# Attention scores in one five-bank tile, the low part of the queries by halves of TensorE's rows

## The chip, the cores and the metric

One core of one Trainium2 chip runs the whole kernel. The metric is the device time of one launch in microseconds (us). The kernel before took 2810.9 us (median of three runs, 2809.32 to 2814.49). The launch that the hardware profiler recorded took 2803.03 us; its span, from the first to the last instruction, is 2801.1 us.

## The reference, cut to what matters

The kernel is one layer of a diffusion backbone: a token mixer (differential attention beside a bidirectional Mamba-2 scan), and after it a mixture of experts. The change lies in the attention and in what stands next to it. There are 1024 latent tokens as queries, 1280 keys (256 context tokens and the 1024), 8 heads, and for each head two softmaxes with keys of 64 numbers:

```python
s = einsum('bqhcd,bkhcd->bchqk', q, k) * ATTN_SCALE      # c: the two softmaxes, d: 64
p = softmax(s, axis=-1)
w = p[:, 0] - lam * p[:, 1]
o = einsum('bhqk,bkhd->bqhd', w, v)                      # d: 128
o = o * rsqrt(mean(o * o) + EPS) * g_subln * (1.0 - lam_init)
...
ya = o_attn @ w_branch_attn
ys = y_ssd @ w_branch_ssd
out = (g_a * ya + g_s * ys) @ w_out
```

All of it is float32. The kernel keeps that accuracy with TensorE's faster fp32r form by splitting a number into a high part (what fp32r holds) and a low part (the rest): a product of two such numbers is taken as high times high, high times low and low times high.

## The kernel before

The program is one long stream that a planner writes when the kernel is built (class `Flow`, from line 106). Every piece of work is a generator that yields what it waits for: tiles, free buffers of a ring, an engine, or a condition. `Flow.run` keeps a modelled clock for each engine and each buffer, and always lets go on the stream with the lowest priority number that could start by then. Each engine then executes its instructions in the order in which they were written; on the chip semaphores guard the data alone. So the modelled durations settle the order, and the chip settles the times.

**Queries and keys (`norm_and_qkv`, `post_qk`).** After the projection, each two token tiles are transposed, split in high and low (`sa`, `sb`), and stored to memory as `qk`, [head and softmax, 128 rows, 2T + NT columns], T = 1024 and NT = 1280. The rows are twice the 64 numbers of a key. The first T columns hold the high part of the queries in both halves, the next T columns their low part in both halves, and the last NT columns the keys: high part in the upper half of the rows, low part in the lower. A query pair of tiles takes eight stores, all from SyncE's queue.

**Attention (`attention`, from line 1342).** A head has eight tiles of 128 queries. `main` goes through 32 pairs of tiles, four to a head, in the order of `PLAN`: `S` is a softmax's scores for one query tile, `t` a group of four transposes of finished weights, `v` a step of the product with the values. A pair's scores run two pairs ahead of its transposes (`LEAD`), and the last two `v` lag by one more.

`scores` computes one softmax of one query tile in three pieces of 512, 512 and 256 keys. Each piece has its own bank from the ring `sps` (four banks), and takes two matmuls over all 128 rows: the queries' high part against the keys (high and low at once, by the two halves of the rows), and their low part against the same. `piece` has VectorE read the bank, scale it and write it to `e`, with the minimum of the piece as a by-product; `soft` joins the three minima (`red`), has ScalarE take the exponential with its sum, and after the second softmax has VectorE do a reciprocal, a small product and the combination of both softmaxes (`stt`, 1280 columns).

`attention_ahead` loads the stored `qk`, one tile of 1664 KB for each softmax of a head, into a ring of three, from GpSimd's queue. A tile goes back to the ring with the last query tile of its head.

**The branch products (`branches`, from line 1194).** The merged projections of both branches are 32 outputs of [128, 512], each a sum of 24 matmuls (8 chunks, three products of parts). The stream has the lowest priority, and so stands wherever the planner saw TensorE wait for something. The first 16 outputs (`ssd`) are spread over the attention: output n is not begun before `PACE[n]` pairs are done. The other 16 (`attn`) need the attention's results, and so come after it. All take their banks from the ring `bacc` (two banks), which `norm`, the attention's own normalisation once a head, uses too. `gated` multiplies an `ssd` output by its gate and stores it; `merge` does so for `attn` and adds the two.

**What follows.** `merge_and_out` zeroes a result buffer by stores from a tile of zeros and does the output projection, the router and the experts.

Names in the profile: `sps<-qk` scores, `e<-sps` VectorE's reads, `tr<-cst,e` transposes, `pv<-wr,vv` the product with the values, `bacc<-bx...` branch products, `bacc<-cst` the normalisation's. Line 147 is the matmul of the helper `mm`, 151 that of `tp`; a line can be a helper's.

Of the kernel before, what the change touches and what calls it, by code (L numbers as in the profile page):

```python
# [19 lines left out]
P = 128  # L20
D = 1024
KC = 8
# [12 lines left out]
PLAN = "S0 t0 v3'|S1 t1 v4' t2|S2 v0 t3 v1|S3 t4 v2"  # L35
# [339 lines left out]
class Layer:  # L375
# [114 lines left out]
    def norm_and_qkv(s):  # L490
# [5 lines left out]
        s.qk = [s.dram(f"qk{j}", [8, P, 2 * T + NT]) for j in range(2)]  # L496
# [163 lines left out]
        def post_qk(ps, kind, j, t):  # L660
# [36 lines left out]
            if two[2] == 2:  # L697
                o0 = (t // 2 - (kind == "q")) * 2 * P
                dst = s.qk[j].rearrange("(m u) (v x) c -> v u x m c", u=2, v=2)
# [494 lines left out]
    def branches(s):  # L1194
# [9 lines left out]
        whs, wls = s.ring(op, [P, 4, P], "bwh", 3, F32R), s.ring(op, [P, 4, P], "bwl", 3, F32R)  # L1204
# [42 lines left out]

        def main():
            for n, (kind, h) in enumerate(todo):
                for m in range(8):  # L1250
                    if kind == "ssd":
                        yield [lambda: st["pairs"] >= PACE[8 * n + m]]
                    yield [acc]
                    b = acc.get()
                    for k in range(KC):
                        yield [lambda: (kind, h, k) in xs and (kind, h, m, k // 4) in ws]
                        (xh, xl), (wh, wl) = xs[kind, h, k], ws[kind, h, m, k // 4]
                        yield [xh, F.ready[_n(xl)] + SLACK[5], wh, wl]
                        s.mm3(b, wh[:, k % 4], wl[:, k % 4], xh, xl, k == 0, k == KC - 1)
                        if k % 4 == 3:  # L1260
                            whs.put(wh)
                            wls.put(wl)
                        if m == 7:
                            xhs.put(xh)
                            xls.put(xl)
                    F.spawn(3, (gated if kind == "ssd" else merge)(h, m, b))

        def gated(h, m, b):
# [6 lines left out]
            acc.put(b)  # L1275
# [3 lines left out]
        def merge(h, m, b):  # L1279
# [9 lines left out]
            acc.put(b)  # L1289
# [34 lines left out]
    def attention_ahead(s, go):  # L1324
# [3 lines left out]
        s.qks, s.heads = s.ring(qp, [P, 2 * T + NT], "qk", 3, F32R), {}  # L1328

        def loads():  # L1330
            yield [go]
            for h in range(8):
                for c in range(2):
# [8 lines left out]
    def attention(s):  # L1342
        tc, nc, F = s.tc, s.nc, s.F
        ap, pp = s.open("at"), s.open("aps", True)
        if True:
            S = s.ring(pp, [P, 512], "sps", 4)
            TR = s.ring(pp, [P, 512], "tr", 1)
            PV = s.ring(pp, [P, 512], "pv", 1)
            acc = s.acc
# [16 lines left out]
            def main():  # L1366
# [5 lines left out]
                for p in range(len(pairs) + LEAD + 1):  # L1372
                    for j in range(4):
# [6 lines left out]
            def scores(h, qp, j, state):  # L1380
# [4 lines left out]
                qt, c = 2 * qp + j // 2, j % 2  # L1385
                if c == 0:
                    yield [es, sts]
                    w = state.setdefault((h, qp), [[], [], [], {}, []])
                    w[0].append(es.get())
                    w[4].append(sts.get())  # L1390
                e, st = state[h, qp][0][-1], state[h, qp][4][-1]
                tq = slice(qt * P, (qt + 1) * P)
                yield [lambda: (h, c) in heads]
                qk = heads[h, c]
                qa, qb, ks = qk[:, :T], qk[:, T:2 * T], qk[:, 2 * T:]
                got = []
# [6 lines left out]
                F.spawn(1, soft(e, st, s0[:, qt:qt + 1], c, got, state[h, qp][1]))  # L1403
                if qt == 7:
                    qks.put(qk)

            def piece(e, m, sps, n, got):
                yield [sps, "DVE"]
                F.ts_reduce(e, sps[:, :n], -0.125, ALU.mult, ALU.min, m)
                S.put(sps)  # L1410
                got.append(1)

            def soft(e, st, s0, c, got, flags):
                yield [lambda: len(got) == 3, "DVE"]
                F.red(st[:, 6 + c:7 + c], st[:, 3 * c:3 * c + 3], ALU.min)
# [57 lines left out]
            def norm(h, ot, s0):  # L1473
                yield [s0, "DVE"]
                F.stt(s0, s0, EPS, s0, ALU.mult, ALU.mult)
                yield [acc]
# [15 lines left out]
                for half in range(2):  # L1492
                    sl = slice(half * 512, half * 512 + 512)
                    yield [F.ready[_n(r)] + SLACK[3], acc]
# [983 lines left out]
```

## Time and profile before

| | |
|---|---|
| median of three runs | 2810.9 us (2809.32 to 2814.49) |
| the profiled execution | 2803.03 us, span 2801.1 us |
| TensorE's matmuls (PE) busy | 2618.4 us, 93% |
| its weight loads (PEld) | 2101.6 us, 75% |
| VectorE (DVE) | 2008.3 us, 72% |
| ScalarE (ACT) | 1339.9 us, 48% |
| GpSimd (POOL) | 888.9 us, 32% |
| mean granted TensorE clock | 0.974 |

Times inside the execution count from the span's start. The attention's scores run from 1053.9 to 1476.4, and the last matmul of the branch products starts at 1633.2. A matmul's duration in the profile is from its start to its modelled end, and holds a tail in which the next one already runs: what it costs on a busy engine is the step from its start to the next start. VectorE's durations overlap in the same way by a little. A group of instructions of one form is printed with its number, the union of their times, the mean of one, and the engine's idle time before them.

### The profile page before, as it was taken

How to read it: one execution, taken by the hardware profiler on the slowest of the kernel's cores; microseconds unless marked ns; L12 is line 12 of the kernel's file. 1: busy time of each engine (PE TensorE's matmuls, PEld its weight loads, DVE VectorE, ACT ScalarE, POOL GpSimd, SP SyncE). 2: the span in 40 equal slices, each digit the busy share in tenths (PEclk: the TensorE clock that was granted, in tenths of full speed). 3: DMA queues.
4: the chain of work that ended last, by engine and by line, in shares of the span. 5: the costliest groups of instructions: out<-in, count | busy, mean ns of one | idle time of the engine just before them, and what ended most of it. 6: DMA issues, size and time to landing. Idle time of an engine off the chain costs nothing. (4 is left out here: it accounts for less than half of the span.)

```text
span 2801.1 us, 41274 instructions
## 1 busy us (share of the span) xinstructions
PE 2618.4 (93%) x14561; PEld 2101.6 (75%) x14561; DVE 2008.3 (72%) x4690; ACT 1339.9 (48%) x2104; POOL 888.9 (32%) x671
## 2 busy tenths in 40 slices
PE   7999999999999999999999999899999998999891
PEld 4888778778787777888887787688878776776660
DVE  6877123768686749888894767877888877788753
ACT  4211123344444546666764422345666665666641
POOL 0111010545353520000000000065666656567641
PEclk9999999999999999999999999999999999999995
DMA  7767253243334354233234953478899999999997
GB/s 279 221 208 214 67 142 105 67 137 91 121 91 132 106 168 149 81 106 131 88 101 135 292 181 142 170 265 248 293 311 315 312 275 278 301 315 315 317 305 202
DMA packets 275123, 544.63 MB, mean 194 GB/s; under 512 B 31531, under 2 KB 166804, under 8 KB 247907
## 3 DMA queue, kind: packets, MB, share of 16 engines
q1 hardware_dynamic: 238754, 435.05, 45.5%
q0 software_dynamic: 36160, 106.93, 15.1%
q8 instruction: 115, 1.88, 0.3%
q14 instruction: 94, 0.76, 0.1%
HBM read 432.73 MB, written 124.73 MB: 199 GB/s over the span
## 5 line engine op out<-in xcount | busy, mean ns | idle before, releaser
L170 DVE TENSOR_TENSOR gl<-raw,gh 128x1024 fp32r<-128x1024 f32 x240 | 288.1, 1218 | 39.4 <-ACT gh L163 39.4
L147 PE MATMUL acc<-hh,hi 128*128 128x512 f32 (+2 forms) x760 | 304.8, 401 | 1.3 <-DVE ux L186 1.3
L163 ACT CAST gh<-raw 128x1024 fp32r<-128x1024 f32 x240 | 247.5, 1050 | 95.7 <-PE gu L147 63.2
L147 PE MATMUL acc<-hl,hi 128*128 128x512 f32 (+2 forms) x760 | 289.4, 381 | 0.0
L147 PE MATMUL acc<-hh,lo 128*128 128x512 f32 (+1 forms) x736 | 281.0, 382 | 3.0 <-DVE lo L170 3.0
L147 PE MATMUL gu<-gh,xh 128*128 128x512 f32 (+3 forms) x672 | 279.5, 416 | 3.3 <-ACT xh L163 3.0
L147 PE MATMUL gu<-gl,xh 128*128 128x512 f32 (+3 forms) x672 | 265.6, 395 | 4.5 <-DVE gl L170 4.4
L147 PE MATMUL gu<-gh,xl 128*128 128x512 f32 (+3 forms) x672 | 265.7, 395 | 0.5 <-DVE xl L170 0.5
L192 DVE TENSOR_SCALAR_CACHE_REDUCE e<-sps 128x512 f32<-128x512 f32 (+1 forms) x384 | 214.4, 597 | 29.5 <-PE sps L147 29.2
L261 POOL DMA_INDIRECT cr<-cumd,crow x98 | 118.9, 1213 | 312.5 <-DVE crow L186 280.9
L267 POOL DMA_INDIRECT yacc<-y,tk x98 | 184.4, 1881 | 84.5 <-issue 31.4
L147 PE MATMUL sps<-qk 128*128 128x512 f32 (+1 forms) x768 | 195.3, 386 | 8.2 <-DVE e L192 4.8
L155 ACT ACTIVATE e<-e,st 128x1280 f32<-128x1280 f32 x128 | 174.8, 1366 | 31.7 <-DVE st L201 31.5
L261 POOL DMA_INDIRECT wc<-wtab,tk x98 | 143.7, 1466 | 137.7 <-DVE tk L181 101.1
L147 PE MATMUL acc<-hi,hh 128*128 128x512 f32 x448 | 181.1, 404 | 0.0
L147 PE MATMUL acc<-hi,hl 128*128 128x512 f32 x448 | 176.1, 393 | 0.4 <-DVE hl L170 0.4
L147 PE MATMUL acc<-lo,hh 128*128 128x512 f32 x448 | 175.8, 392 | 0.0
L147 PEld LDWEIGHTS sps<-qk 128*128 128x128 f32 x768 | 140.9, 191 | 40.8 <-DVE e L192 9.8
L147 PEld LDWEIGHTS acc<-hh,hi 128*128 128x128 f32 (+1 forms) x760 | 142.5, 187 | 32.7 <-issue 4.2
L147 PE MATMUL pv<-wr,vv 128*128 128x256 f32 x640 | 164.2, 380 | 0.0
L147 PEld LDWEIGHTS acc<-hh,lo 128*128 128x128 f32 x736 | 138.8, 189 | 32.8 <-DVE lo L170 4.0
L147 PEld LDWEIGHTS acc<-hl,hi 128*128 128x128 f32 (+1 forms) x760 | 142.6, 188 | 27.4 <-issue 0.8
(326 smaller groups left out, 6254.8 us busy)
## 6 DMA issues: line engine op xcount, KB each, us to landing
raw<-in_w_e_gate_dram SPq DMA_DIRECT2D x64, 1024.0 KB, 8.6
raw<-in_w_e_up_dram SPq DMA_DIRECT2D x64, 1024.0 KB, 12.4
draw<-in_w_e_down_dram SPq DMA_DIRECT2D x64, 1024.0 KB, 10.8
qk<-qk POOLq DMA_DIRECT2D x16, 1664.0 KB, 11.1
raw<-in_w_in_dram SPq DMA_DIRECT2D x40, 512.0 KB, 4.7
wada<-in_w_ada_dram SPq DMA_DIRECT2D x32, 512.0 KB, 5.5
R<-acd SPq DMA_DIRECT2D x64, 256.0 KB, 5.3
qk<-sa SPq DMA_DIRECT2D x52, 256.0 KB, 4.0
```

The costliest lines, as they stand in the source:

```text
L147: s.nc.tensor.matmul(out, l, r, start=start, stop=stop)
L155: s.nc.scalar.activation(out, in_, fn, **kw)
L163: s.nc.scalar.copy(out, in_)
L170: s.nc.vector.tensor_tensor(out, a, b, op=op)
L192: s.nc.vector.tensor_scalar(out, a, s1, None, op0=op0, op1=op1, accum_out=acc)
L261: s.nc.gpsimd.indirect_dma_start(out=out, out_offset=None, in_=table, in_offset=bass.IndirectOffsetOnAxis(ap=idx, axis=0), **kw)
L267: s.nc.gpsimd.indirect_dma_start(out=table, out_offset=bass.IndirectOffsetOnAxis(ap=idx, axis=0), in_=in_, in_offset=None, compute_op=ALU. ...
```

## The change

The scores of both softmaxes of a query tile are computed together, in one tile of five banks [128, 2 NT], and there is only one such tile. `PLAN` has two `S` a pair in place of four.

- The store to memory changes. The high part of the queries still stands in both halves of the rows. The keys of the first softmax are stored high above low, those of the second low above high. The queries' low part is stored once, in a buffer of its own, `qb`: the first softmax's in the upper 64 rows, the second's in the lower. A query pair takes five stores in place of eight.
- The low part of the queries is now multiplied by the keys' high part alone. For 1024 of the 1280 keys of each softmax that is two matmuls over 64 rows, the first softmax's on the upper half of TensorE's rows and the second's on the lower, issued in turn to different banks (`PIECES`). The other 256 keys of each (`TAILS`), which share the middle bank, go over all 128 rows with keys from `kz`, a small tile whose other half is zero.
- VectorE reads 1280 columns at once, with one minimum, and `red` is gone. The tile is free after the second read.
- GpSimd loads five tiles a head in place of two: `qb` (512 KB, ring of two), two pieces of `kz` (64 KB each), and two of `qk` (now 1152 KB each, ring of three). Both `qk` tiles of a head go back with its last scores.
- The ring `bacc` has one bank. After the last scores the five banks are given up, and a new ring `bacc2` of four serves the `attn` products and the last normalisations. The first three `attn` outputs are taken over chunks 0 to 6 first, and their last chunk, which is head 7, follows.
- The branch weights have four buffers each in place of three, and the tile of zeros has 256 columns, read twice by each store.

```diff
-PLAN = "S0 t0 v3'|S1 t1 v4' t2|S2 v0 t3 v1|S3 t4 v2"
+PLAN = "S0 t0 v3' t1 v4' t2|S1 v0 t3 v1 t4 v2"
+TAILS = 1024, 0
+PIECES = (0, 0), (1, 256), (0, 512), (1, 768)
...
-                for w, v, o in ((a, 0, 0), (a, 1, 0), (b, 0, T), (b, 1, T)) if kind == "q" else ((a, 0, 2 * T), (b, 1, 2 * T)):
-                    for u in range(2):
-                        F.dma(dst[v, u][:, :, o + o0:o + o0 + 2 * P], w[64 * u:64 * u + 64].bitcast(F32).rearrange("x (m c) -> x m c", m=4))
+                for u in range(2):
+                    wa, wb = (w[64 * u:64 * u + 64].bitcast(F32).rearrange("x (m c) -> x m c", m=4) for w in (a, b))
+                    if kind == "q":
+                        for v in range(2):
+                            F.dma(dst[v, u][:, :, o0:o0 + 2 * P], wa)
+                    else:
+                        F.dma(dst[u, u][:, :, T + o0:T + o0 + 2 * P], wa)
+                        F.dma(dst[1 - u, u][:, :, T + o0:T + o0 + 2 * P], wb)
+                if kind == "q":
+                    F.dma(low[:, :, o0:o0 + 2 * P], b.bitcast(F32).rearrange("x (m c) -> x m c", m=4))
...
-        s.acc = acc = s.ring(pp, [P, 512], "bacc", 2)
+        s.acc, s.acc2 = s.ring(pp, [P, 512], "bacc", 1), None
...
+            yield [lambda: s.acc2 is not None]
+            first = []
+            for m in range(3):
+                yield [s.acc2]
+                first.append(s.acc2.get())
+                yield from product(first[m], "attn", 0, m, range(7))
+            for n in range(16):
+                if n < 3:
+                    b = first[n]
+                else:
+                    yield [s.acc2]
+                    b = s.acc2.get()
+                yield from product(b, "attn", n // 8, n % 8, range(7 if n < 3 else 0, 8))
+                F.spawn(3, merge(n // 8, n % 8, b))
...
+                for c in range(2):
+                    F.swdma(s.kz[c][h % 2][64 * c:64 * c + 64], s.qk[h // 4][2 * (h % 4) + c, 64 * c:64 * c + 64, T + TAILS[c]:T + TAILS[c] + 256])
...
-            S = s.ring(pp, [P, 512], "sps", 4)
+            S = s.ring(sp, [P, 2 * NT], "sps", 1)
...
-                for i, (k0, n) in enumerate(((0, 512), (512, 512), (1024, 256))):
-                    yield [S, qk]
-                    sps = S.get()
-                    F.mm(sps[:, :n], qa[:, tq], ks[:, k0:k0 + n], True, False)
-                    F.mm(sps[:, :n], qb[:, tq], ks[:, k0:k0 + n], False, True)
-                    F.spawn(1, piece(e[:, c, k0:k0 + n], st[:, 3 * c + i:3 * c + i + 1], sps, n, got))
+                yield [S, *qk, qb, s.kz[0][h % 2], s.kz[1][h % 2]]
+                sps = S.get()
+                for c, k0 in enumerate(TAILS):
+                    o = sps[:, c * NT + k0:c * NT + k0 + 256]
+                    F.mm(o, qk[c][:, tq], qk[c][:, T + k0:T + k0 + 256], True, False)
+                    F.mm(o, qb[:, tq], s.kz[c][h % 2], False, True)
+                for c, k0 in PIECES:
+                    F.mm(sps[:, c * NT + k0:c * NT + k0 + 512], qk[c][:, tq], qk[c][:, T + k0:T + k0 + 512], True, False)
+                for c, k0 in PIECES:
+                    half = slice(64 * c, 64 * c + 64)
+                    F.mm(sps[:, c * NT + k0:c * NT + k0 + 512], qb[half, tq], qk[c][half, T + k0:T + k0 + 512], False, True, 118.0)
+                F.spawn(1, soft(e, st, s0[:, qt:qt + 1], sps, w[1], (h, qt) == (7, 7)))
...
+            def soft(e, st, s0, sps, flags, last):
+                for c in range(2):
+                    yield [sps, "DVE"]
+                    F.ts_reduce(e[:, c], sps[:, c * NT:c * NT + NT], -0.125, ALU.mult, ALU.min, st[:, 6 + c:7 + c])
+                    F.spawn(1, power(e, st, c, s0, flags))
                 S.put(sps)
+                if last:
+                    s.close("sps", flush=False)
+                    s.acc2 = s.ring(s.open("fps2", True), [P, 512], "bacc2", 4)
```

## Rows read from the trace of the kernel before

**Rows 1.** Busy time of each engine by stretch (count), granted clock, DMA share, GB/s.
```profile
1054.00:1080.00 26.00, 20.90 (x76) 13.98 (x75) 24.82 (x78) 14.69 (x22) 1.30 (x1) 0.87 0.45 145
1080.00:1478.00 398.00, 394.26 (x2254) 344.27 (x2253) 358.09 (x1145) 274.06 (x452) 13.83 (x20) 1.00 0.30 103
1530.00:1640.00 110.00, 100.49 (x414) 78.32 (x414) 72.05 (x110) 45.55 (x76) 0.00 (x0) 0.97 0.88 284
```
**Rows 2.** TensorE's groups by shape, 1080 to 1478 us: busy us, mean ns, idle before.
```profile
L147 PE MATMUL pv<-wr,vv 128*128 128x256 f32 x592 | 152.2, 380 | 0.0
L147 PE MATMUL sps<-qk 128*128 128x512 f32 x473 | 148.0, 432 | 3.1 <-DMA qk<-qk 3.0
```
**Rows 3.** VectorE's groups by shape, the same stretch.
```profile
L186 DVE SCALAR_TENSOR_TENSOR e<-e,st 128x1280 f32<-128x1280 f32 x60 | 93.1, 1552 | 2.1
```
**Rows 4.** Timeline of TensorE within the attention: start us, us, instructions.
```profile
1205.49 1.03 PE L147 MATMUL pv<-wr,vv 128*128 128x256 f32 x4
1206.17 1.50 PE L147 MATMUL sps<-qk 128*128 128x512 f32 x6
1207.51 0.60 PE L151 MATMUL tr<-cst,e 128*128 128x128 f32 x4
1207.94 1.03 PE L147 MATMUL pv<-wr,vv 128*128 128x256 f32 x4
...
1211.83 0.39 PE L147 MATMUL bacc<-bxl,bwh 128*128 128x512 f32 x1
1212.06 0.40 PE L147 MATMUL bacc<-bxh,bwl 128*128 128x512 f32 x1
```
**Rows 5.** Timeline of VectorE within the attention.
```profile
1200.99 0.68 DVE L192 TENSOR_SCALAR_CACHE_REDUCE e<-sps 128x512 f32<-128x512 f32 x1
...
1201.60 0.69 DVE L192 TENSOR_SCALAR_CACHE_REDUCE e<-sps 128x512 f32<-128x512 f32 x1
...
1202.21 0.42 DVE L192 TENSOR_SCALAR_CACHE_REDUCE e<-sps 128x256 f32<-128x256 f32 x1
...
1202.56 0.16 DVE L205 RECIPROCAL st<-st 128x1 f32<-128x1 f32 x1
...
1204.53 0.74 DVE L186 SCALAR_TENSOR_TENSOR ot<-ot,gsub,bacc 128x512 f32<-128x512 f32 x1
```
**Rows 6.** Timeline of TensorE in the experts, around transposes over 64 rows.
```profile
2313.84 0.39 PE L147 MATMUL gu<-gh,xl 128*112 128x512 f32 x1
2314.16 0.46 PE L151 MATMUL xt<-cst,xg 64*128 64x64 f32 x4
2314.55 0.50 PE L147 MATMUL gu<-gh,xh 128*128 128x512 f32 x1
2314.89 0.39 PE L147 MATMUL gu<-gl,xh 128*128 128x512 f32 x1
```
**Rows 7.** Timeline of TensorE in the experts, around products in four column groups.
```profile
1844.35 0.39 PE L147 MATMUL gu<-gh,xl 128*128 128x512 f32 x1
1844.66 1.07 PE L147 MATMUL dn<-draw,hh 128*32 128x256 f32 x16
1845.66 0.50 PE L147 MATMUL gu<-gh,xh 128*128 128x512 f32 x1
```
**Rows 8.** Timeline of TensorE in the attention's first stretch.
```profile
1062.56 4.16 PE L147 MATMUL sps<-qk 128*128 128x512 f32 x12 [2.03 <-DVE e L192]
```
**Rows 9.** DMA issues, 1094.5 to 1095.2 us: count, KB, us to landing.
```profile
qk<-qk POOLq DMA_DIRECT2D x1, 1664.0 KB, 7.5
```
**Rows 10.** Waits, 1080 to 1478 us: total us, times, longest us.
```profile
PE sps L147 <- DMA qk<-qk: 3.0, 5, 0.9
```
**Rows 11.** Timeline of VectorE after the attention: a gated branch output.
```profile
1513.36 0.69 DVE L170 TENSOR_TENSOR braw<-bacc,braw 128x512 f32<-128x512 f32 x1 [0.72 <-PE bacc L147]
```
**Rows 12.** DMA issues, 1035 to 1500 us: count, KB each, median us to landing.
```profile
braw<-gt SPq DMA_DIRECT2D x12, 256.0 KB, 2.6
```
**Rows 13.** Waits, 1530 to 1600 us.
```profile
PE bacc L147 <- ACT bxh L163: 6.8, 5, 3.5
```

More of the change, by code (lines that the diff above doesn't have):

```diff
@@ L495, in norm_and_qkv @@
         wada = I["w_ada"][0].rearrange("(p k) c -> p k c", p=P)
-        s.qk = [s.dram(f"qk{j}", [8, P, 2 * T + NT]) for j in range(2)]
+        s.qk = [s.dram(f"qk{j}", [8, P, T + NT]) for j in range(2)]
+        s.qb = [s.dram(f"qb{j}", [4, P, T]) for j in range(2)]
         s.vv = [s.dram(f"vv{j}", [NT, 4, P]) for j in range(2)]
@@ L1246, in weights, with product @@
                         F.spawn(3, half(rv, hi, lo, lambda q=(kind, h, m, a), v=(hi, lo): ws.update({q: v})))
-        def main():
[L1249 to L1266, printed above, removed]
+        def product(b, kind, h, m, ks):
+            for k in ks:
+                yield [lambda: (kind, h, k) in xs and (kind, h, m, k // 4) in ws]
+                (xh, xl), (wh, wl) = xs[kind, h, k], ws[kind, h, m, k // 4]
+                yield [xh, F.ready[_n(xl)] + SLACK[5], wh, wl]
+                s.mm3(b, wh[:, k % 4], wl[:, k % 4], xh, xl, k == 0, k == KC - 1)
+                if k % 4 == 3:
+                    whs.put(wh)
+                    wls.put(wl)
+                if m == 7:
+                    xhs.put(xh)
+                    xls.put(xl)
@@ new lines, in main @@
+        def main():
+            for n in range(16):
+                yield [lambda: st["pairs"] >= PACE[n]]
+                yield [s.acc]
+                b = s.acc.get()
+                yield from product(b, "ssd", n // 8, n % 8, range(8))
+                F.spawn(3, gated(n // 8, n % 8, b))
+            yield [lambda: s.acc2 is not None]
[4 more added lines that the diff above has]
+                yield from product(first[m], "attn", 0, m, range(7))
+            for n in range(16):
+                if n < 3:
[5 more added lines that the diff above has]
+                F.spawn(3, merge(n // 8, n % 8, b))
@@ L1327, in attention_ahead @@
         qp = s.open("qks", side="right")
-        s.qks, s.heads = s.ring(qp, [P, 2 * T + NT], "qk", 3, F32R), {}
+        s.qks, s.heads = s.ring(qp, [P, T + NT], "qk", 3, F32R), {}
+        s.qbs = s.ring(qp, [P, T], "qb", 2, F32R)
+        s.kz = [[qp.tile([P, 256], F32R, name=f"kz{c}{i}") for i in range(2)] for c in range(2)]
+        for c in range(2):
+            for i in range(2):
+                F.fill(s.kz[c][i][64 - 64 * c:128 - 64 * c].bitcast(F32), 0.0)
         def loads():
@@ L1372, in main @@
                 for p in range(len(pairs) + LEAD + 1):
-                    for j in range(4):
+                    for j in range(2):
                         for op in plan[j].split():
@@ L1403, in scores @@
-                F.spawn(1, soft(e, st, s0[:, qt:qt + 1], c, got, state[h, qp][1]))
-                if qt == 7:
[L1405 to L1409, printed above, removed]
+                qt = 2 * qp + j
+                yield [es, sts]
+                w = state.setdefault((h, qp), [[], [], [], {}, []])
+                e, st = es.get(), sts.get()
+                w[0].append(e)
@@ new lines, in scores @@
+                tq = slice(qt * P, (qt + 1) * P)
+                yield [lambda: (h, 1) in heads]
+                qk, qb = [heads[h, c] for c in range(2)], heads[h, 2]
+                yield [S, *qk, qb, s.kz[0][h % 2], s.kz[1][h % 2]]
[4 more added lines that the diff above has]
+                    F.mm(o, qb[:, tq], s.kz[c][h % 2], False, True)
@@ L1410, in piece @@
+            def soft(e, st, s0, sps, flags, last):
+                for c in range(2):
+                    yield [sps, "DVE"]
+                    F.ts_reduce(e[:, c], sps[:, c * NT:c * NT + NT], -0.125, ALU.mult, ALU.min, st[:, 6 + c:7 + c])
+                    F.spawn(1, power(e, st, c, s0, flags))
                 S.put(sps)
[L1411 to L1415, printed above, removed]
+                if last:
+                    s.close("sps", flush=False)
+                    s.acc2 = s.ring(s.open("fps2", True), [P, 512], "bacc2", 4)
@@ L1416, in soft, with power @@
+            def power(e, st, c, s0, flags):
                 yield [st, "ACT"]
@@ L1515, in attention @@
             F.run(lambda: s.st["heads"] == 8)
-            s.close("at", "aps", "qks")
+            s.close("at", "qks")
     def ada_late(s, pool, pm):
@@ L1615, in merge_and_out @@
         got = []
-        zero = pg.tile([P, 512], F32, name="zero")
+        zero = pg.tile([P, 256], F32, name="zero")
         F.fill(zero, 0.0)
```

34 lines of the change are left out of this document (15 added, 19 removed).

## The prediction

> **What bounds the kernel now.** I read the busy time by stretch first. In the attention's steady part TensorE is busy 394.3 of 398 us at full clock, VectorE 358.1 [rows 1]. TensorE's groups by shape come next: its idle time before scores and products there is 3.1 us in all [rows 2]. So the matmuls set this stage's time, and VectorE, 90% busy, is close behind. The count of the combining operation gives the pace: 60 query tiles in 398 us, 6.63 us a tile [rows 3].
>
> What a matmul costs I take from the timeline, as steps from start to start. A branch matmul of 512 columns steps by 0.23 [rows 4], one of 256 by half of that, 0.115. A softmax's scores are four of 512 and two of 256: 1.15. Product group and scores together take 2.02 (1205.49 to 1207.51), so a product group takes 0.87; a transpose group takes 0.43 (1207.51 to 1207.94) [rows 4].
>
> VectorE's timeline gives a read of 512 at 0.61 and of 256 at 0.35, so 0.26 for each further 256. The block after a tile's second exponential (reciprocal, small product, combination) takes 1.97, from 1202.56 to 1204.53 [rows 5].
>
> The ring of four banks lets TensorE run up to four pieces ahead of VectorE's reads. The branch products fill what waits the planner foresees. The stage is saturated on one engine, and the change takes away work of that engine but also the slack between it and its neighbour.
>
> **The change part by part.** I sum against the profiled execution, 2803.0 us, and move the sum to the median, 2810.9, by the same difference.
>
> *Scores, the work taken away.* Before, a query tile has eight matmuls of 512 and four of 256: 8 x 0.23 + 4 x 0.115 = 2.30. After it has four of 512 and four of 256 over all rows, 1.38, and four of 512 over half the rows. If two halves run side by side these are 2 x 0.23 = 0.46, the tile takes 1.84, and 64 tiles save 64 x 0.46 = 29.4 us. If they don't, they take 0.92 and nothing is saved. No row shows two row halves at once. The nearest shows column groups: 16 matmuls of 256 columns in four groups take 1.00 us, from 1844.66 to 1845.66 [rows 7], where even at 0.115 they would take 1.84 one by one. I take the full overlap, 29.4, with 0 as the other end.
>
> *Scores, what the halves cost.* Around four transposes over 64 rows the experts' timeline shows the price of going there and back [rows 6]. The first of them starts 0.32 after a matmul that is worth 0.23: 0.09 to enter. The next full matmul starts 0.39 after it, where four transposes of half the usual columns are worth half of 0.43, 0.22: 0.17 to leave. The full matmul after it steps by 0.34: 0.11 more. The entry to column groups is 0.31, 0.08 over the step [rows 7]. Every score tile enters and leaves once. Here a transpose or a product group follows, not a split matmul, so I leave out the 0.11; of the 0.17 I keep 0.13, since 512 columns cover a weight load that 64 columns don't. That is 0.22 a tile, 14.1 us over 64. The ends are 0.09 for the entry alone (5.8) and 0.37 for all of it (23.7).
>
> The Trainium skill, "TensorEngine Tiling (Array Packing)", Key Properties, states that changing the tiling mode drains TensorE. By that rule the change pays twice a tile, and rows 6 agrees, with 0.09 at the entry and 0.17 at the exit. Without the rule the sum would be 14.1 us better.
>
> *One score tile.* The next tile's first matmul waits for both reads of the one before. A read of 1280 is 0.35 + 4 x 0.26 = 1.39 [rows 5], two are 2.78, and the last matmul's tail adds 0.39 - 0.23 = 0.16 [rows 4]: 2.94 if VectorE is free at once. By the new order TensorE has three transpose and two product groups between the pair's first and second tile, 3 x 0.43 + 2 x 0.87 = 3.03, and two and three, 3.47, before the next pair's first. That is 0.09 and 0.53 of room. When the 1.97 block stands ahead of the reads, TensorE waits up to 1.88 or 1.44; behind it stand the transposes, products and branch matmuls, since the engine keeps the order. Against that, VectorE's own work falls: 3.14 a tile before (4 x 0.61 + 2 x 0.35), 2.78 after, and two `red` are gone. From 6.0 of 6.63 it comes to about 5.5. Where the planner models such a wait it puts branch matmuls in it, 0.69 for a chunk of three. It prices the halves at 0.118 and no switch, so on the chip TensorE is later than it believes, and VectorE has that much more time. I take 3 us; the ends are 0 and 64 x 1.66 = 106 us (the mean of 1.88 and 1.44), of which filler takes what there is.
>
> *The start.* The first tiles have no transposes between them. Before, TensorE waited there for VectorE, 5.1 of 26 us idle at a mean clock of 0.87, and after a wait of 2.03 us twelve score matmuls took 4.0 us where full steps give 2.3 [rows 1, 8]. After, a tile takes 1.84 + 0.22 + 2.94 = 5.0 us in turn with its reads, against 4.8 of VectorE's work alone, so five such turns lose 1 us; at half clock the scores add 1.8 in each. I take +1, ends -2 and +9.
>
> *One bank for the `ssd` outputs.* After the attention the last of them run back to back on two banks. With one, the next waits for the tail and for the gating, 0.16 + 0.69 [rows 4, 11], about 0.85. Four such joins after the last product step: +3. If the gate's load, 2.6 [rows 12], is issued only after the output, +13. The lower end is 0, where other work covers it.
>
> *Head joins.* Before, the second `qk` tile of the next head came 0.9 us late at most, 3.0 in all [rows 10]; it landed 7.5 us after its issue for 1664 KB [rows 9]. Now both tiles are freed at the head's end, and 1152 KB land in 5.2 (by size) to 7.5. TensorE has 3.47 us there and a foreseen wait, which branch chunks fill (a head has eight, 5.5 us). GpSimd's queue issues this load first, then the next head's other four; nothing else is queued there but the values' load. I take 0 against before; ends -3 and 7 x (7.5 - 3.47) = 28, where filler is lacking.
>
> *At nothing.* The 24 stores fewer lie under the projections; if SyncE held those up it would be a gain of some us at most. The first three `attn` outputs ahead of head 7: after the attention TensorE waits for the split chunks as they arrive, 6.8 us [rows 13], and that wait is for chunks 0 to 6 too, so it stays; ends -4 and +2. The fourth weight buffer holds what these three keep. The zeros' stores are waited for by nobody before the experts.
>
> Sum: -29.4 + 14.1 + 3 + 1 + 3 = -8.3 us: 2794.7 for the profiled execution, 2802.6 beside the median.
>
> **The rivals.**
>
> *The reads of the one tile set the pace (slower).* Place: the first transposes after each tile, at the next tile's first matmul. For it speaks the room of 0.09, and VectorE at 5.5 of 6.4 us a tile; against it the lighter VectorE and the filler. If the 1.97 block stands ahead in every fourth tile, 16 x 1.97 = 31.5, less one chunk each, 16 x 0.69 = 11: +20.5. With -15.3 for the scores and +4 for start and bank that is +9.2: 2820. It decides from a mean wait of (15.3 - 4) / 64 = 0.18 us a tile.
>
> *The switches are nearly free.* If only the entry's 0.09 is paid and TensorE never waits for the tile: -29.4 + 5.8 + 3 = -20.6: 2790. For it: 512 columns hide weight loads better than 64. Against it: the exit of 0.17 [rows 6].
>
> *The halves overlap in part.* If a pair takes 0.30, a third of the way from 0.23 to 0.46, a tile saves 0.32, in all 20.5: -20.5 + 14.1 + 7 = +0.6: 2811.5. For it: rows 7 shows column groups only. The Trainium skill, "TensorE: Matmul & The Clock Gate", Measured speedup vs the span model, gives 3.07 for four row groups at once; scaled to two, as an estimate, that is 0.30 a pair. No run so far shows it.
>
> *The halves don't overlap at all,* so that the change doesn't do what it says: 14.1 + 7 = +21: 2832. Against it: four column groups do overlap [rows 7].
>
> **How the numbers follow.** What a measurement can tell from no change is 0.2%, 5.6 us. The forecast has 0.36, its own range 2796 to 2809, and of it 0.26 lies below 2805.3 and 0.10 within the bound. The reads 0.27 (0.21 slower, 0.06 within). Free switches 0.17, all faster. Partial overlap 0.14 (0.02, 0.08, 0.04). No overlap 0.06, all slower. Faster 0.45, same 0.24, slower 0.31. The range, 2787 to 2828, reaches past the free switches and past the reads at +9, with room for a start at half clock; a failed overlap and the worst of the reads stay out.
>
> **What would show it.** Pairs of half-row score matmuls should start a few ns apart and pairs 0.23 apart; the next full matmul about 0.13 late. VectorE's reads should be 64 x 2 of 1280 at about 1.4 a step. TensorE's idle time before `sps` by VectorE should stay under 5 us in the steady part, and the score tiles should come every 6.4 us. I am wrong if halves step by 0.23 each, if a visit costs over 0.4, or if the waits for `e` before `sps` come to over 11 us.

## The result and the profile after

The changed kernel takes 2877.6 us (2872.5 to 2883.5, 4 runs), the kernel before 2810.1 beside it (2808.6 to 2814.5): ratio 1.0235 [1.0213, 1.0256], 67 us slower. I had forecast 2803, with 2787 to 2828 as the range. The profiled execution of after is 2883.5 us long.

The first row compares with the first of [rows 1], the second with the second: busy time of each engine by stretch (PE, PEld, DVE, ACT, POOL), granted clock, DMA share, GB/s. The stretches are cut near the same events, the attention's start and its steady part.
```profile
1050.00:1099.00 49.00, 31.89 (x127) 22.35 (x125) 23.54 (x34) 17.12 (x25) 4.82 (x4) 0.79 0.42 139
1099.00:1562.00 463.00, 420.70 (x2280) 321.60 (x2280) 327.00 (x540) 275.14 (x452) 24.81 (x39) 0.96 0.28 90
```
In the second stretch TensorE was busy 394 of 398 us before and is busy 421 of 463 now, VectorE 327 of 463. No engine is full any more; waits set the pace. The start has become 19 us longer (first score to first product of values, 29.1 to 47.7), the rest up to the last score 68 us. Part of this comes back afterwards, since 14 of the 16 `ssd` outputs are done by then, and before it was not quite 10. From 1050 us to the end of the last branch matmul it is 583.6 us before and 653.8 after. Of the 70 us, 51 are idle time of TensorE (18.6 to 69.8) and 19 are matmuls that take longer. The granted clock over that stretch is 0.94, before it was 0.99; 5% of 584 us is some 29 us, as an estimate, from which the 11 us go off that the halves save (below). Behind that stretch the profiled execution of after takes 1178 us and that of before 1167; the traces of r1, r2, r3 and r5, whose code is the same there, take 1163 to 1183, so I count no part of it as the change's.

TensorE's waits, 1050 to 1720 us (total us, times, longest us), beside [rows 10]:
```profile
PE sps L149 <- DVE e L194: 31.6, 21, 5.1
PE bacc L153 <- DVE rs_y L188: 13.2, 3, 4.4
PE bacc L153 <- DVE braw L172: 5.4, 2, 2.7
PE sps L149 <- DMA qk<-qk: 4.4, 3, 2.5
```
Two waits have grown: the scores wait for VectorE's reads (4.8 us before, all of it in the start; now 13.2 of the 31.6 are there), and the norm's matmuls into `bacc` wait at the heads' ends.

The first wait is seen on VectorE's timeline of a pair's second tile (compare [rows 5]), and on TensorE's of the same tile and the next:
```profile
1159.85 1.49 DVE L194 TENSOR_SCALAR_CACHE_REDUCE e<-sps 128x1280 f32<-128x1280 f32 x1 [3.36 <-PE sps L149]
...
1161.26 0.16 DVE L207 RECIPROCAL st<-st 128x1 f32<-128x1 f32 x1
...
1161.76 1.55 DVE L188 SCALAR_TENSOR_TENSOR e<-e,st 128x1280 f32<-128x1280 f32 x1
1163.23 1.48 DVE L194 TENSOR_SCALAR_CACHE_REDUCE e<-sps 128x1280 f32<-128x1280 f32 x1
```
```profile
1159.07 0.73 PE L149 MATMUL sps<-qk,qb 64*128 64x512 f32 x4
1159.73 1.13 PE L149 MATMUL pv<-wr,vv 128*128 128x256 f32 x4
...
1164.92 0.39 PE L149 MATMUL bacc<-bxl,bwh 128*128 128x512 f32 x1
1165.15 0.40 PE L149 MATMUL bacc<-bxh,bwl 128*128 128x512 f32 x1
1165.38 0.28 PE L149 MATMUL sps<-qk 128*128 128x256 f32 x1
```
The block of the tile before (reciprocal to combination, 1.97 us) stands not ahead of the two reads but between them: 3.38 us lie between their starts instead of 1.41. So it is in all 32 second tiles of a pair (3.38 to 4.70), and in no first. The tile comes free 1.97 us later, and the planner, which foresees it, puts branch matmuls there: the idle time is 42 us in the steady stretch, but score tiles within a head are mostly 6.4 to 7.9 us apart, in turn short and long (1157.60 to 1165.38 is 7.78), where the mean was 6.63 before with the joins in it.

The second wait lies at a head join, where TensorE goes from one head's tiles to another's. At the end of head 0:
```profile
1178.82 1.05 PE L149 MATMUL bacc<-cst,dg 128*128 128x1 f32 x8
1184.28 1.09 PE L153 MATMUL bacc<-cst,rs_y 128*128 128x128 f32 x4 [4.41 <-DVE rs_y L188]
1186.21 1.12 PE L153 MATMUL bacc<-cst,rs_y 128*128 128x128 f32 x4 [0.84 <-DVE ot L188]
1186.97 0.56 PE L149 MATMUL sps<-qk 128*128 128x256 f32 x1
```
Head 0's last product ended at 1155.2, but an `ssd` product had the one bank from 1154.9 to 1171.7. The norm's sums come at 1177 to 1179, then TensorE is idle for its inverse root, because the next scores (head 2) wait for the output buffer `ot`, of two, that this norm gives back. Those scores then run at half rate: four of 512 take 1.84 us (1187.98 to 1189.82) instead of 1.0. At five of the seven joins the score tiles start 14 to 15 us apart; before it was 5.7 to 8.8 at all of them.

### The profile page after: what moved, and what is told of

It reads as the page before. It is cut to its first block, busy times and chain, and to the rows that moved or that the text cites. A ratio compares the mean times of both kernels' runs of the same rounds, so it can differ in the third digit from the quotient of the medians.

```text
span 2881.8 us, 40644 instructions
## 1 busy us (share of the span) xinstructions
PE 2643.3 (92%) x14561; PEld 2073.1 (72%) x14561; DVE 1972.6 (68%) x4050; ACT 1340.3 (47%) x2104; POOL 912.6 (32%) x699
## 4 chain that ended last, share of the span: by engine, by line
PE 50%; DVE 13%; DMA 13%; issue 4%; ACT 3%; POOL 2%; SPq 1%; POOLq 0%; DVEq 0%; ACTq 0%
PE gu L149 13%; PE acc L149 9%; PE dn L149 7%; PE sps L149 5%; PE bacc L149 4%; PE pv L149 3%; DMA yacc<-y,tk 3%; DMA cr<-cumd,crow 2%; DVE e L194 2%; PE tr L153 2%; PE xt L153 2%; PE aux L149 2%; DMA raw<-in_w_e_up_dram 2%; DVE G L188 2%; DVE gl L172 1%
## 5 line engine op out<-in xcount | busy, mean ns | idle before, releaser
L194 DVE TENSOR_SCALAR_CACHE_REDUCE e<-sps 128x1280 f32<-128x1280 f32 x128 | 188.1, 1487 | 117.5 <-PE sps L149 117.5
L263 POOL DMA_INDIRECT wc<-wtab,tk x98 | 137.3, 1401 | 139.7 <-DVE tk L183 95.1
L165 ACT COPY wr<-tr 128x512 f32<-128x512 f32 x160 | 93.3, 583 | 173.5 <-PE tr L153 172.2
L263 POOL DMA_INDIRECT xg<-htab,tk x98 | 128.2, 1308 | 109.2 <-PE xt L153 47.7
```

What stands on the lines that cost most here:

```text
L165: s.nc.scalar.copy(out, in_)
L194: s.nc.vector.tensor_scalar(out, a, s1, None, op0=op0, op1=op1, accum_out=acc)
L263: s.nc.gpsimd.indirect_dma_start(out=out, out_offset=None, in_=table, in_offset=bass.IndirectOffsetOnAxis(ap=idx, axis=0), **kw)
```

## The experiments

Theory A: the one tile's loop of scores and reads, with the block inside, makes the loss. Theory B: the one bank delays the norm and stalls the head joins. Rivals: the halves' switches, and work merely moved. The table gives the median, the ratio to the kernel before on the same chip, and, from TensorE's trace between 1050 us and the end of the last branch matmul, its idle time and all else (before: 18.6 and 565.0; after: 69.8 and 584.1).

| run | us | ratio, 95% | idle | rest |
|---|---|---|---|---|
| r1_reads_together | 2849.8 | 1.0157 [1.0122, 1.0193] | 50.6 | 575.2 |
| r2_third_ot | 2846.9 | 1.0133 [1.0097, 1.0170] | 48.6 | 570.9 |
| r3_full_rows | 2885.6 | 1.0287 [1.0252, 1.0322] | 65.6 | 589.5 |
| r4_before_one_bank | 2884.3 | 1.0279 [1.0243, 1.0315] | 67.1 | 589.6 |
| r5_together_and_ot | 2821.8 | 1.0072 [1.0048, 1.0096] | 38.3 | 567.3 |
| r6_both_full_rows | 2829.1 | 1.0100 [1.0076, 1.0125] | 42.2 | 575.9 |
| r7_before_one_bank_ot | 2843.2 | 1.0165 [1.0131, 1.0198] | 46.0 | 577.6 |
| r8_before_third_ot | 2800.1 | 1.0003 [0.9988, 1.0018] | 19.6 | 561.3 |
| r9_norm_elsewhere | 2867.8 | 1.0250 [1.0220, 1.0280] | 67.6 | 587.5 |
| r10_norm_and_together | 2855.3 | 1.0198 [1.0175, 1.0222] | 50.0 | 580.3 |
| r11_norm_together_ot | 2852.5 | 1.0195 [1.0171, 1.0218] | 45.9 | 584.5 |
| r12_before_norm_elsewhere | 2818.4 | 1.0081 [1.0056, 1.0106] | 33.4 | 568.1 |
| r13_norm_first | 2814.1 | 1.0064 [1.0050, 1.0078] | 35.4 | 565.9 |
| r14_norm_first_early | 2819.8 | 1.0084 [1.0072, 1.0097] | 35.5 | 566.5 |

The kernel before took 2795.8 to 2810.2 us, by the chip, so I compare ratios; 0.0036 is 10 us.

**r1, the two reads side by side**
```diff
-                for c in range(2):
-                    yield [sps, "DVE"]
+                yield [sps, "DVE"]
+                for c in range(2):
```


> The changed kernel with one difference: both reads of a score tile stand next to each other on VectorE, so the block of the tile before (reciprocal, small product, combination, 1.97 us) can no longer run between them. In the changed kernel it does so in 32 of 64 tiles (3.39 us between the starts of the two reads instead of 1.41). Theory A, the one score tile sets the pace, and the block between its reads makes most of the loss: 32 x 1.98 = 63 us less holding, of which the idle time after VectorE and the clock lost with it come back: 2825 to 2840 us, TensorE's idle before the scores by VectorE from 31.6 to under 12 us. Theory B, the head joins on the one bank for the ssd outputs make most of it: 2865 to 2878 us, the joins' gaps of 5.2 us stay. Theory D, the time went into other work planned into the gaps (branch products), which only moves: 2870 to 2880 us.


No block stands between reads now, and the steady tiles come every 6.5 us. The wait for `e` falls from 31.6 to 3.1, as A had it. But the time falls by 0.8% only, half of what A promised, because the joins grow (the row's columns as above):
```profile
PE bacc L153 <- DVE ot L188: 11.6, 6, 6.1
PE bacc L149 <- DVE braw L172: 8.0, 3, 4.0
PE bacc L153 <- DVE rs_y L188: 5.1, 2, 2.6
PE sps L149 <- DVE e L194: 3.1, 1, 3.1
```
From a head's last tile's reads to the next head's first scores it is now 10 to 17 us, where it was 7 to 8 at most of them. So A alone doesn't explain the loss, but its wait is real.

**r2, a third output buffer**
```diff
-            s0s = s.ring(ap, [P, 8], "s0", 3)
+            s0s = s.ring(ap, [P, 8], "s0", 4)
-            ots = s.ring(ap, [P, T], "ot", 2)
+            ots = s.ring(ap, [P, T], "ot", 3)
```


> The changed kernel with a third buffer for a head's attention output (ot) and a fourth for its sums (s0): the first scores of the head after next no longer wait for the norm of a head, which in the changed kernel comes late, because the one bank of the ssd outputs is held by a product when the head ends. Theory B, this wait makes the head joins (gaps of 5.2 us on TensorE in the norm, and half clock after them): the gaps of 5.2 us go, and 25 to 40 us with them, 2838 to 2853 us. Theory A, the pace of the score tile is most of the loss: 12 to 20 us less, 2857 to 2866 us, since the tile after a join waits for VectorE anyway.


The gaps of 5.2 us are gone and the waits for `rs_y` with them, the clock in the steady part is 1.00 again, and the time is within B's numbers. The waits for `e` stay (34.5 us). **r8** gives the kernel before the same buffers:

> The kernel before, its two banks kept, with the third output buffer alone: the control for the runs with that buffer. Before has 1 to 3 us of TensorE idle at the joins in all, so 2806 to 2811 us, the same as before within 0.2%. If the buffer gives the same 30 us here as in the changed kernel, it has nothing to do with the one bank: 2780 us.


Nothing changes there (2800.1 us, ratio 1.0003), so the buffer is worth something only with the late norm.

**r4, the kernel before with one bank**
```diff
-        s.acc = acc = s.ring(pp, [P, 512], "bacc", 2)
+        s.acc = acc = s.ring(pp, [P, 512], "bacc", 1)
+        s.acc1 = s.ring(pp, [P, 512], "bacc1", 1)
...
+                    r = s.acc1 if kind == "attn" and m % 2 == 0 else acc
```


> The kernel before with one difference: inside the attention the ssd products and the norms share one bank instead of two (the second bank serves only the attention's branch products afterwards, in turn with the first). Theory B: the norm comes late at the head joins as in the changed kernel: 20 to 35 us slower than before, 2830 to 2845 us, with gaps of about 5 us on TensorE at most head joins. Theory A: the bank alone costs little with the ring of four score banks, which keeps TensorE fed: 2810 to 2818 us.


This alone loses as much as the whole change does, and more than even B expected. TensorE at the first head's end:
```profile
1146.66 0.39 PE L147 MATMUL bacc<-bxh,bwl 128*128 128x512 f32 x1
1150.05 1.02 PE L147 MATMUL bacc<-cst,dg 128*128 128x1 f32 x8 [2.99 <-DVE braw L170]
1151.85 1.87 PE L147 MATMUL bacc<-cst,dg 128*128 128x1 f32 x8 [0.78 <-ACT dg L155]
1153.98 0.80 PE L147 MATMUL bacc<-bxh,bwh 128*128 128x512 f32 x1 [0.26 <-DVE s L186]
...
1161.27 0.39 PE L147 MATMUL bacc<-bxh,bwl 128*128 128x512 f32 x1
1162.44 0.65 PE L151 MATMUL bacc<-cst,rs_y 128*128 128x128 f32 x4 [0.79 <-DVE braw L170]
1163.93 0.65 PE L151 MATMUL bacc<-cst,rs_y 128*128 128x128 f32 x4 [0.84 <-DVE ot L186]
1164.34 1.42 PE L147 MATMUL sps<-qk 128*128 128x512 f32 x6
```
The norm waits for the gating of a product (2.99). While it works out its inverse root, a whole next product of 24 matmuls takes the bank (1153.98 to 1161.27), and only then come the broadcasts and the next scores, 23 us after the scores before them. So it is at six of the seven joins: the score tiles start 26 us apart, once 34.

**r7 and r12** take this kernel apart: r7 with r2's buffers, r12 with the norm's sums and broadcasts in the bank of the transposes.
```diff
-                yield [acc]
-                ps = acc.get()
...
+                    yield [F.ready[_n(o2)] + SLACK[4], TR]
+                    ps = TR.get()
...
+                    yield [F.ready[_n(r)] + SLACK[3], TR]
+                    pb = TR.get()
```


> The kernel before with one shared bank for the ssd products and the norms (2884.3 us), and with a third buffer for a head's attention output and a fourth for its sums. If what makes the joins long there (25 us between two heads' tiles, with a whole ssd product of 24 matmuls between the norm's sums and its broadcasts) is that the next scores wait for the output buffer that the norm gives back: 2808 to 2820 us. If it is the bank itself (products and norms one behind the other on TensorE whatever the buffers): 2850 us or more.

> The kernel before with one bank for the ssd products inside the attention (2884.3 us with the norms on it too), and the norm in the transposes' bank. Theory B, the loss there is the norm shut out by products: back to 2800 to 2815 us. If one bank for the ssd products alone costs (each product waits for the gate's read of the one before, some 2 us, and with the third buffer that kernel still took 2843 us): 2830 to 2845 us.


Both times lie between their two forecasts, and neither edit brings back the whole: 46 us (1.0165) and 23 us (1.0081) remain of 78. Norm and products shutting each other out are most of it; about 23 us remain with one `ssd` bank and the norm in another's.

**r3, all 128 rows again**
```diff
...
+                for c, k0, n in [(c, k0, 256) for c, k0 in enumerate(TAILS)] + [(*q, 512) for q in PIECES]:
+                    o, ks = sps[:, c * NT + k0:c * NT + k0 + n], qk[c][:, 2 * T + k0:2 * T + k0 + n]
+                    F.mm(o, qk[c][:, tq], ks, True, False)
+                    F.mm(o, qk[c][:, T + qt * P:T + qt * P + P], ks, False, True)
```


> The changed kernel with the low-part pass over all 128 rows again (12 matmuls a tile, 2.30 us, the q and k storage of the kernel before, the products of two low parts with it), all else as in the changed kernel: one five-bank tile, two reads of 1280, one bank for the ssd outputs. If the halves' price of switching (0.35 us a tile, 64 tiles) makes part of the loss, this kernel is faster than the changed one by 5 us or more. If the halves save what their rows show (2.13 against 2.30 us a tile, 11 us over 64 tiles) and that reaches the end: 2885 to 2892 us. If the tile's loop of scores and reads sets the pace, each tile's scores are in that loop, and it comes out the same way, 2883 to 2892 us; if the pace is set by the planner's filling of the loop, 2875 to 2882 us.


Slower than after by 8 us, or 0.0052 in the ratio, which is 15; the intervals just meet. The halves are no part of the loss.

**r5 and r6, both repairs, with halves and without** (the diffs of r1 and r2; r6 adds that of r3).

> The changed kernel with both differences at once: the two reads of a tile next to each other on VectorE, and a third buffer for the head's attention output (fourth for its sums). Each alone took some 28 to 31 us off (2849.8 and 2846.9 against 2877.6 us). Theory A+B, two losses in different places: with the reads apart the steady tiles take 7.40 us (from the run with the third buffer), with the reads together 6.55 us between the joins (from the other run), so 2846.9 - 57 x 0.85 = 2798 us, range 2790 to 2815, no gap over 2 us at a head join. Rival, the two hide each other (what the pace gives back is lost again in the joins, as the run with the reads together showed with 10 to 17 us between a head's last tile and the next): 2825 to 2847 us.

> The kernel of the run with both differences (reads together, third ot), but with the low-part pass over all 128 rows again (2.30 us of matmuls a tile instead of 2.13). If TensorE sets the end again once both losses are gone, the halves' saving shows now: 64 x 0.17 = 11 us slower than that kernel, between 7 and 15. If the loop of scores and reads on the one tile still sets the pace (2.13 or 2.30 + 2.94 + 0.2 us, less than the 6.4 us of TensorE's work a tile), the same 11 us would show only where a read ends last: 0 to 5 us slower. If the halves' switches cost more than their rows show: faster.


r5 gives back 46 of 67 us by the ratios, short of the 80 that A and B together promised; 2821.8 lies just under the rival's range. r6 is 7 us slower, at the low edge of the numbers; the intervals overlap, but TensorE's time apart from waits grows by 8.6 us, near the 64 x 0.17 = 11.

**r9 to r11, the norm in the transposes' bank** (r12's edit on after; r10 with r1's, r11 with r1's and r2's)

> The changed kernel with the head's norm taken off the ssd outputs' bank: its sums and broadcasts go through the bank of the transposes, in four short holds, the sums read in two halves. Nothing else differs, the reads are apart, two output buffers. Theory B, the norm waits for the ssd product that holds the one bank: no gap over 3 us at the head joins, and about what the third output buffer gave, 2838 to 2852 us. If the third buffer helped for another reason (more heads in flight), and the norm's own work (squares, inverse root, broadcasts, 5 us from the squares to the broadcasts) makes the join: 2865 to 2878 us.

> The changed kernel with the norm in the transposes' bank and the two reads of a tile next to each other, two output buffers. The run with the reads together and a third buffer still had 38 us of TensorE idle against 19 before, with one join of 8.5 us and several small ones where the norm waited for the bank. Theory A+B: without that wait the joins go to what they are before, and the time to 2798 to 2810 us. If the rest lies in the start and in the lower clock, not in the joins: 2815 to 2824 us, as with the third buffer.

> The same with the third output buffer too. If the norm off the bank has removed the wait for the buffer, the buffer gives nothing more: the same as without it within 0.2%. If the scores of the head after next still wait for it: 5 us or more faster.


r9 is as slow as after: B's numbers miss, and the rival's, for the norm's own work, hold. r10 misses both of its forecasts, and r10 and r11 are slower than r5. r11 is as r10 within 0.2%, as forecast for the case that the norm off the bank has removed the wait for the buffer. The waits of r9 show what it cost:
```profile
PE sps L149 <- DVE e L194: 31.0, 19, 5.1
PE tr L153 <- DVE ot L188: 9.6, 10, 2.0
PE tr L153 <- DVE s L188: 8.5, 9, 1.8
```
The norm now comes on time (its sums at 1163 instead of 1177), but its sums and broadcasts take turns with the transposes in their one bank: the transposes wait 13.9 us and the broadcasts 4.2, in all 18 where the waits for `bacc` had been 23 (13.2, 5.4, and 4.2 for `ot`). The scores stand behind the transposes in the written order. The conflict has moved to another ring, so these three don't separate B from the norm's own work; r4 and r12 do, in which that work is the same and only the bank differs.

**r13 and r14, the norm first**
```diff
-                yield [lambda: st["pairs"] >= PACE[n]]
+                yield [lambda: st["pairs"] >= PACE[n] and st["heads"] >= min(st["pairs"] // 4, 7)]
```
Both are r5 with a rule; r14 has `(st["pairs"] + 1) // 4`.

> The kernel with the reads together and a third output buffer (1.0072 of before), and a rule for the one bank: no ssd product starts while the norm of a finished head is still to come. If the joins that are left there (a gap of 4.4 us ahead of a norm, one join of 8.5 + 3.8 us, some small ones, 10 us of TensorE's idle in all) come from products that take the bank ahead of a norm: 8 to 14 us less, 2808 to 2814 us where the other takes 2822 us (1.002 to 1.005 of before). If a product that is already running when the head ends is what holds the bank: within 4 us of it.

> The same, with the rule from three quarters of a head on: no ssd product starts once three of the four pairs of a head are done and until its norm has come, so that hardly any product is running when the norm comes. If running products hold the bank: 8 to 14 us less than the kernel without a rule (1.002 to 1.005 of before), and less than with the later rule. If the ssd work that this moves behind the attention is missing as a filler of TensorE between the score tiles: slower than with the later rule by 5 us or more.


The norm's waits for `bacc` are gone in r13, all but 1.7 us behind the last head, yet it gains only 0.0008 over r5, within the intervals. Its time lies at the edge of the first forecast, its ratio outside. r14 takes 5.7 us more than r13, which speaks for the missing filler, but the profiled executions agree to the last branch matmul (602.0 and 601.3 us), so it isn't shown. r13's longest waits:
```profile
PE sps L149 <- DMA qk<-qk: 13.9, 8, 2.7
PE bacc L149 <- ACT bxh L165: 9.7, 4, 4.1
PE sps L149 <- DVE st L207: 3.9, 2, 3.1
```
With those waits gone another shows: at six joins a head's first tile waits 1.2 to 2.7 us for its second `qk` tile, 10.2 us in all, where it was 3.0 before [rows 10]; the other 3.8 us lie at the attention's start. From 1050 us on that is 10 of the 16.8 us of idle time that r13 has over before. I read this from the waits; no run takes them away.

**r15 and r16, do the halves overlap?** Both are r5 with one edit, run once each: 2814.4 us beside 2795.8, and 2865.8 beside 2810.2.
```diff
-PIECES = (0, 0), (1, 256), (0, 512), (1, 768)
+PIECES = (0, 0), (0, 512), (1, 256), (1, 768)      # r15
-                    half = slice(64 * c, 64 * c + 64)
+                    half = slice(0, 64)                # r16
```


> The kernel with the reads together and a third output buffer, with the order of the half-row matmuls changed from half 0, half 1, half 0, half 1 to half 0, half 0, half 1, half 1. In the alternating order the two of a pair start 3 ns apart and the next pair 0.33 us after it, 0.10 later than a full matmul's step of 0.226. If a half-row matmul overlaps only with a neighbour on the other half: two steps of 0.23 to 0.33 between those on the same half, and one pair 3 ns apart in the middle, the four in 0.75 to 0.9 us instead of 0.66. If the 0.10 is a weight load that can't run beside matmuls on the same rows, the second on the same half starts 0.3 us or more after the first.

> The kernel with the reads together and a third output buffer, with all four half-row matmuls of a tile on half 0 (the second softmax's low part then takes the rows of half 0 too, so its values differ; nothing else does). With the order half 0, half 0, half 1, half 1 the rows of the trace were the same as in turn: two starts 2 to 7 ns apart, the next two 0.33 us later, 0.66 us from the first start to the matmul that follows the four, so the starts in the trace do not show which of them ran side by side. If halves on different rows do run side by side: here, where none can, the four take 4 x 0.213 = 0.85 us or more (0.9 with a step of 0.226), 0.2 us a tile more than in turn, and the tile 2.3 us or more. If a matmul of 64 rows is simply shorter whatever its neighbour (0.166 each): 0.66 us again, and what the change calls side by side saves nothing by it.


TensorE's timeline of one low-part pass and what follows it, in r5, r15 and r16:
```profile
1140.17 0.73 PE L149 MATMUL sps<-qk,qb 64*128 64x512 f32 x4
1140.84 0.70 PE L149 MATMUL pv<-wr,vv 128*128 128x256 f32 x2
```
```profile
1137.95 0.74 PE L149 MATMUL sps<-qk,qb 64*128 64x512 f32 x4
1138.62 0.70 PE L149 MATMUL pv<-wr,vv 128*128 128x256 f32 x2
```
```profile
1146.14 1.21 PE L149 MATMUL sps<-qk,qb 64*128 64x512 f32 x4
1147.28 0.48 PE L149 MATMUL pv<-wr,vv 128*128 128x256 f32 x1
```
Four on the same rows take 1.14 us to the next matmul, the two halves 0.67 in either order. r16 comes out as forecast for halves side by side, r15 in neither of its two ways. So halves do run side by side, and it is worth 0.47 a tile, 30 us over 64, against four on one half; r16's time apart from waits is 34 us longer than r5's. On the same rows the steps are 0.34, 0.24, 0.24 and 0.32: the first and the last carry some 0.1 each, so that is a price of going to half rows and back, and not of a weight load at every matmul.

## Why the prediction was wrong

**What bounds the kernel** was read rightly: TensorE, with little slack beside it. The change moved the bound to waits. By the ratios the two steps that failed, the bank and the one tile, make 46 of the 67 us (r5).

**Scores, the work taken away.** Held: the halves overlap (r16). The tile fell from 2.30 to 2.13 us and not to 2.06.

**What the halves cost.** Under-sized but within its ends. The first half enters 0.09 late (0.32 after a matmul of 0.23), the second pair starts 0.33 after the first, 0.10 late, the next matmul 0.32 after that, another 0.09, and what follows steps 0.06 (transposes) to 0.10 late. That is 0.35 a visit against my 0.22; the ends were 0.09 and 0.37. The Trainium skill, "TensorEngine Tiling (Array Packing)", Key Properties, has each change of mode drain the engine; these rows agree, at both ends of the visit. That leaves 0.17 a tile, 11 us, less the last item, which the next operation pays: 0.07 to 0.11, 4 to 7 us. r6 measures 7, r3 8 to 15.

**One score tile.** This step failed in its place and its price. I had the block ahead of both reads now and then (in every fourth tile, for the rival) and took 3 us. In the trace it stands between them in every second tile, 32 x 1.97 = 63 us of holding. I worked from the order of the work and missed that a stream which waits again after its first read lets an older stream's block in. Taking that away gives 0.8% alone (r1), and 0.6% with the joins repaired (r2 to r5), 17 to 22 us. My own sign, under 5 us of waits for `e` in the steady part, came out at 18.4. The rival "the reads of the one tile set the pace" named this wait, with every fourth tile and 2820; by r1 it is about a third of the loss.

**The start.** +1 became +19, past my end of +9. The block between the reads makes TensorE idle 5.1 us twice, and the scores after it run at half rate (1.84 us to the half-row matmuls). A wait that I left out is the one for the second softmax's `qk` tile, 2.5 us, which a tile of both softmaxes needs from the start:
```profile
1054.86 0.58 PE L149 MATMUL sps<-qk 128*128 128x256 f32 x1 [2.50 <-DMA qk<-qk]
...
1070.39 0.55 PE L149 MATMUL sps<-qk 128*128 128x256 f32 x1 [5.07 <-DVE e L194]
...
1071.38 1.91 PE L149 MATMUL sps<-qk 128*128 128x512 f32 x4
1073.22 1.22 PE L149 MATMUL sps<-qk,qb 64*128 64x512 f32 x4
```
With the reads together (r5) it is 37.9 us instead of 47.7 from first score to first product, +9, at my end.

**One bank for the `ssd` outputs.** This step is the main error. I priced it after the attention, +3 for four joins of 0.85, and there it is right: r13 shows 2.6 us for three. I never asked who else used the two banks during the attention. The norm of each head did, and the head after next waited for it: r4 shows 78 us for this edit alone in the kernel before, r2 29 us by the ratios for the wait's removal in the changed one (24 from r1 to r5).

**Head joins.** I counted the `qk` load and took 0 against before, with an end of +28. In the changed kernel it is 0.6 us at the joins instead of 3.0, since other waits cover it; in r13, where they are gone, 10.2, or +7. That the step's value held was luck: it held only through a stall that I hadn't seen.

**At nothing.** From the first of the 16 `attn` outputs to the end of the last it is 102.9 us instead of 103.7, as costed.

**What is left open.** r13 is still 18 us over before: 16.8 us more idle time, of which `qk` loads are 10. TensorE's matmuls, at 565.9 us against 565.0, show nothing of the halves' saving; I put that down to the granted clock, 0.97 over that stretch against 0.99 (2% of 566 us is some 11 us, as an estimate), which no run separates. No version here beats the kernel before.

## What to carry to other kernels

When a ring is cut, list every stream that takes from it and who waits behind each; price the edit in the stage where two of them meet, not only where one runs back to back. A consumer that waits twice for one tile lets other work in between, and holds the whole tile for it. When one wait is taken away, look for the next in the same place: here the joins hid the loads, and the pace hid the joins.

## What the runs showed of the hardware

The trace's starts don't show which half-row matmuls run side by side. They stand in pairs 2 to 10 ns apart also where the program gives two on the same rows one after the other (r15), and the four take the same 0.67 us. My sign for the overlap ("pairs start a few ns apart") was weaker than I thought; it is the time to the next matmul, with and without a free other half (0.67 and 1.14), that shows it. That the order makes no difference suggests that a matmul starts ahead of an earlier one on other rows. The Trainium skill, "TensorE: Matmul & The Clock Gate", The mechanism ("What overlaps and what doesn't"), has matmuls start and end strictly in program order. By that, as an estimate from r16's steps, r15's four would take one step of 0.24 more than in turn, 0.9 us. The trace has 0.67, so it doesn't agree; the reordering itself is argued, not shown.
